# Which engine sums the channel blocks of the modulation vectors: one vector of a phase or all of them on the vector engine, and six raw buffers for seven

## The chip, the core and the metric

The kernel runs on one core of a Trainium2 chip. The core has five engines, each with an instruction stream of its own that it works through in order: PE (TensorE, matrix products into the accumulators in PSUM), DVE (VectorE) and ACT (ScalarE) (element-wise work), POOL (GpSimd), and SP (SyncE, which issues the transfers here). They wait for each other by semaphores. The metric is the device time of one launch in microseconds (us).

## What is computed

One denoising step of a two-layer network on 128 context tokens and 128 latent tokens with 1024 channels. All weights come from HBM once, some 300 MB. Per layer:

```python
x += 1/2 * gate1 * swiglu_1(mod1(rms_norm(x)))      # ffn1
u  = mod2(rms_norm(x)); z = u @ w_in                # mixer: attention, 2-D DFT, mLSTM on z,
x += gate2 * ((gated sum of the three branches) @ w_out)   # gates from u @ w_branch_gate
x += 1/2 * gate3 * swiglu_2(mod3(rms_norm(x)))      # ffn2

def adaln(cvec, w, b):                              # where shift, scale and gate come from
    m = jax.nn.silu(cvec) @ w + b                   # w: 1024 x 9216 per layer
    return jnp.split(m, 9, axis=-1)                 # nine vectors of 1024 channels
```

`adaln` is worked out for two condition vectors, one for the context tokens and one for the latent ones ("two groups" below). A modulation vector (layer l, number m) is therefore a product of a 2 x 1024 matrix with a 1024 x 1024 slice of `w_ada`, 4 MB of weights for two rows of result. There are 18 of them. The first two (shift and scale of the first phase) are worked out at the start and are not touched here; the other 16 are spread over the six phases, 3, 3, 3, 3, 3 and 1.

## The kernel before

**Steps and units.** The program is a list of steps that is written out by hand. A *unit* is a block of weights of 128 x 1024 numbers (some of 128 x 768). Products are made from two parts of each weight, so ACT rounds a unit to its high part (`whi`, line 1493) and DVE subtracts to get the low part (`wlo`, line 1494); that is the *split* of a unit. A step of PE takes one unit: 24 products of 256 columns (`mm3`, lines 168 to 170). There are six buffers for split units (`N_SPLIT`), and the executor at the end of the kernel writes, after each step, the split of the unit six further on: its buffer is free once PE is done with the unit of that step. Between steps DVE also multiplies the two halves of SwiGLU (line 655), makes the low part of the result (line 180), and in the mixer does most of the three branches ("lanes").

**Raw buffers.** Weights land in raw buffers of 1 MB (`N_RAW`, seven). SP issues the transfer of a block as soon as a buffer is given back; a block of weights is given back when both of its units are split.

**The modulation vectors.** `mod_steps` makes the steps for the vectors of one phase, and `spread_into` puts them evenly between two places of the step list. The steps of a phase lie in the first part of an ffn (products with `w_ffn_in`) and, in the mixer, between the second product of the first branch and the output product. Two ways are used:

- on PE (12 of the 16 vectors): a raw block of 2 x 128 channels by 1024 columns goes into the products as it is; four products of 512 columns run side by side, each into 32 rows of one PSUM tile (`pd`). One step takes two such blocks; a vector is two steps.
- on DVE (4 of the 16, one in each ffn, list `on_ve`): DVE multiplies a row block of 128 channels by the condition's number of that channel (one per partition, `cT`) and adds it to an accumulator (line 337 for the first block, line 339 for the other seven), one instruction for each group, 512 columns wide. Two halves of the columns make 16 pairs of instructions. Then PE sums the 128 partitions with a one-hot matrix (`hot`) in a step called `total`, one for each half.

After the last step of the phase ACT copies the PSUM tile (`adaev`), a step `post` transposes it and DVE adds the bias and makes gate, scale and shift.

Modulation steps carry no unit: where one stands between two unit steps, everything behind it on its engine waits until it is done. `acc[0]` is the accumulator; in the vector's last pair DVE writes it for the last time, and the products of `total` cannot start before that.

Units are numbered below over the whole program, in the order in which PE takes them: "behind unit 22" is the place after the 22nd unit that PE works through.

Of the kernel before, what the change touches and what calls it, by code (L numbers as in the profile page):

```python
# [17 lines left out]
P = 128  # L18
D = 1024
# [14 lines left out]
N_RAW = 7  # L34
N_SPLIT = 6
N_BLK = 17
N_T2 = 6
BRANCHES = (1, 0, 2)
CT = 8
HOT = 10  # L40
LAG = 2
# modulation vectors that each phase works out: those the vector engine sums first, and the others
ADA = {(0, "ffn1"): ([(0, 4)], [(0, 2), (0, 3)]),
       (0, "mixer"): ([], [(0, 7), (0, 6), (0, 5)]),
       (0, "ffn2"): ([(1, 1)], [(0, 8), (1, 0)]),
       (1, "ffn1"): ([(1, 4)], [(1, 2), (1, 3)]),
       (1, "mixer"): ([], [(1, 7), (1, 6), (1, 5)]),
       (1, "ffn2"): ([(1, 8)], [])}
# [31 lines left out]
def _pack(inputs):  # L80
    """Short vectors side by side, 128 wide, and the per-head gate biases and stabilisers."""
# [43 lines left out]
def trunk_kernel(ctx: ExitStack, tc: tile.TileContext, a: dict):  # L125
# [58 lines left out]
    # ---------------------------------------------------------------- small inputs  # L184
# [22 lines left out]
    # ---------------------------------------------------------------- persistent  # L207
# [36 lines left out]
    # ---------------------------------------------------------------- start-up  # L244
# [38 lines left out]
    def busy(n):  # L283
        """Products of nothing, which bring the tensor engine to its full clock while it has no data."""
        t = pb([P, 512])
        for _ in range(n):
            mm(t, zeros[:, 0:P], zeros)
# [10 lines left out]
    # ---------------------------------------------------------------- modulation  # L298
    def mod_steps(mods_):
        """Products of some modulation vectors.  # L300

        Four products run side by side: two quarters of the channels, two terms of their sums.
        Vector i takes the rows 2 i and 2 i + 1 of each. The vector engine first sums the channel
        blocks of those of the first list, one term per group, and the products sum its lanes."""
        on_ve, on_pe = mods_
        n_ve, mods_ = len(on_ve), on_ve + on_pe
        st = {"left": 4 * len(on_pe) + 2 * n_ve}
        seq = []

        def side(tiles, f0, f1):  # L310
            first = "ps" not in st
            if first:
                st["ps"] = pd([P, 512])
            st["left"] -= 1
            for q, (x, w) in enumerate(tiles):
                mm(st["ps"][32 * q:32 * q + 32, f0:f1], x, w, start=first, stop=st["left"] == 0)
            if st["left"] == 0:
                st["ev"] = t2([P, 512], "adaev")
                ac.copy(st["ev"], st["ps"])

        for i, (l, m) in enumerate(on_ve):
            for r in range(2):
                acc = []
                for jj in range(2):
                    f0 = m * D + r * 512
                    ch = Chunk(a["w_ada"][l, jj * 512:(jj + 1) * 512, f0:f0 + 512], 4, 512)
                    for e in range(4):
                        u = Unit(ch, e, e + 1, 0, 512, split=False)

                        def fn(u=u, k=4 * jj + e, acc=acc):  # L330
                            w = u.raw()[:, 0, :]
                            if k == 0:
                                acc.append(blk([P, 2, 512], "acc"))
                            for g in range(2):
                                c, x = cT[:, k, CT + g:CT + g + 1], acc[0][:, g, :]
                                if k == 0:
                                    ve.tensor_scalar(x, w, c, None, op0=ALU.mult)
                                else:
                                    ve.scalar_tensor_tensor(x, w, c, x, op0=ALU.mult, op1=ALU.add)  # L339

                        seq.append(((2 * i + r) * 8 + 4 * jj + e + 0.5, fn, [u]))

                def total(i=i, r=r, acc=acc):
                    side([(hot[:, HOT - 2 * i - g:HOT - 2 * i - g + 32], acc[0][:, g, c * 256:c * 256 + 256])
                          for g in range(2) for c in range(2)], r * 256, r * 256 + 256)

                seq.append(((2 * i + r) * 8 + 7.5 + LAG, total, []))
        span = 16 * n_ve if n_ve else 1
        for i, (l, m) in enumerate(on_pe):
            for j2 in range(2):  # L350
                us = []
                for j in range(2 * j2, 2 * j2 + 2):
                    ch = Chunk(a["w_ada"][l, j * 256:(j + 1) * 256, m * D:(m + 1) * D], 2, D)
                    us.append(Unit(ch, 0, 2, 0, D, split=False))

                def fn(us=us, i=n_ve + i, j2=j2):
                    for j, u in enumerate(us, 2 * j2):
                        raw = u.raw().rearrange("p e (r c f) -> p e c r f", r=2, c=2)
                        side([(cT[:, 2 * j + e, CT - 2 * i:CT - 2 * i + 32], raw[:, e, c])
                              for e in range(2) for c in range(2)], 0, 512)  # L360

                seq.append(((4 * i + 2 * j2 + 0.4) * span / (4 * len(on_pe)), fn, us))
        seq.sort(key=lambda x: x[0])
        out = [x[1:] for x in seq]

        def post():
# [3 lines left out]
            n = 2 * len(mods_)  # L370
            half = tmp([P, 2, 4, n], "mhalf", bufs=1)
            full = tmp([P, KD, n], "mfull", bufs=1)
            tq = t.rearrange("p c (q x) -> p q c x", x=32)[:, :, :, 0:n]
            ve.tensor_copy(half, tq[:, 0:2])
            for c in range(2):
                o = full.rearrange("p (r c b) x -> p c r b x", r=2, c=2)[:, c]
                i = (x.rearrange("p (r b) x -> p r b x", r=2) for x in (half[:, c], tq[:, 2 + c]))
                ve.tensor_add(o, *i)
            for i, (l, m) in enumerate(mods_):
                o, x = mods[l, m], full[:, :, 2 * i:2 * i + 2]  # L380
                bT = parT[l][:, m * KD:(m + 1) * KD].unsqueeze(2).to_broadcast([P, KD, 2])
                ve.tensor_add(o, x, bT)
                if m % 3 == 1:
                    k0 = 72 + m // 3 * KD
                    gT = parT[l][:, k0:k0 + KD].unsqueeze(2).to_broadcast([P, KD, 2])
                    ve.scalar_tensor_tensor(o, o, 1.0, gT, op0=ALU.add, op1=ALU.mult)
                elif m % 3 == 2 and m != 5:
                    ve.tensor_scalar(o, o, 0.5, None, op0=ALU.mult)
# [4 lines left out]
    # ---------------------------------------------------------------- norms  # L393
    class Norm:
        """Statistics and scaled copies of the residual, block by block.
# [1164 lines left out]
```

## Time and profile before

| | |
|---|---|
| median of 3 runs | 1375.77 us (1375.19 to 1377.95) |
| span of the profiled execution, first to last instruction | 1375.9 us |
| PE busy | 1351.3 us (98%) |
| DVE busy | 915.0 us (67%) |
| ACT busy | 682.3 us (50%) |
| DMA: moved, mean rate | 303.68 MB, 221 GB/s |
| mean granted TensorE clock | 0.990 of full speed |
| DVE, accumulating modulation vectors (lines 337 and 339) | 128 instructions, 85.9 us |
| PE, modulation products from raw weights in the phases | 384 rows of 512 columns, 46.2 us |

The profiled execution has no time of its own beside its span; the span lies inside the range of the timed runs. A product in full precision is two rows of the profile, so the four side-by-side products of a block are eight rows. Busy shares are averages over phases that differ: in the mixer DVE serves the branches as well as the splits, in the second half of an ffn it has little to do. The rows show a matmul as about 0.28 us long while the next starts about 0.12 us later, so durations of PE are read from starts, not from sums.

### The profile page before, as it was taken

What the parts mean: (1) busy time and instruction counts of PE and PEld (TensorE: products, weight loads), DVE (VectorE), ACT (ScalarE), POOL (GpSimd) and SP (SyncE); (2) the same over time, 40 slices, a digit from 0 to 9 for tenths busy, and PEclk for the clock granted to TensorE, in tenths of its full rate; (3) what the DMA queues carried; (4) which work ended last, traced back from release to release, by engine and by line L of the source; (5) the groups of instructions that cost most, each with busy time, mean ns of one, the idle gap of its engine ahead of it and who ended that gap; (6) DMA issues with size and microseconds to landing.
All of it is one profiled execution on the core that took longest, in us unless ns stands there. A gap on an engine that the chain in (4) does not pass through costs nothing.

```text
span 1375.9 us, 26101 instructions
## 1 busy us (share of the span) xinstructions
PE 1351.3 (98%) x10915; PEld 1268.7 (92%) x10916; DVE 915.0 (67%) x1440; ACT 682.3 (50%) x1096; POOL 113.0 (8%) x138
## 2 busy tenths in 40 slices
PE   6999999999999999999999999999999999999998
PEld 4999899888998999999998999998899899999998
DVE  4576755876557589666568666667665668887653
ACT  4544444666544466444455444546564445744442
POOL 2000001300000030000020000130000001200000
PEclk8999999999999999999999999999999999999999
DMA  9999856564468847886639876748445895487520
GB/s 293 333 345 340 260 174 213 159 195 138 157 238 298 272 154 267 300 269 212 206 124 321 305 257 197 204 130 241 154 137 195 297 304 186 147 264 233 192 85 31
DMA packets 247526, 303.68 MB, mean 221 GB/s; under 512 B 5537, under 2 KB 212657, under 8 KB 247409
## 3 DMA queue, kind: packets, MB, share of 16 engines
q1 hardware_dynamic: 245728, 296.98, 66.4%
q0 software_dynamic: 1680, 5.05, 1.1%
q8 instruction: 85, 1.39, 0.4%
q14 instruction: 33, 0.26, 0.1%
HBM read 297.80 MB, written 3.15 MB: 219 GB/s over the span
## 4 chain that ended last, share of the span: by engine, by line
PE 90%; DVE 6%; ACT 2%; DMA 1%; issue 1%; SPq 1%; POOL 0%; ACTq 0%; DVEq 0%
PE pm L168 26%; PE pm L170 25%; PE pm L169 25%; PE pd L165 5%; PE pb L165 2%; DVE wlo L1494 2%; DVE v L498 2%; DVE ul L180 1%; PE pm L752 1%; PE pm L754 1%; PE pm L753 1%; ACT whi L1493 1%; PE pa L165 1%; DMA raw<-w_ada 1%; PE pa L173 1%
## 5 line engine op out<-in xcount | busy, mean ns | idle before, releaser
L1494 DVE TENSOR_TENSOR wlo<-raw,whi 128x1024 fp32r<-128x1024 f32 (+1 forms) x424 | 507.3, 1204 | 326.4 <-ACT whi L1493 316.8
L1493 ACT CAST whi<-raw 128x1024 fp32r<-128x1024 f32 (+1 forms) x424 | 433.9, 1031 | 364.3 <-PE pm L169 253.4
L168 PE MATMUL pm<-uh,whi 128*128 128x256 f32 x1928 | 554.7, 288 | 0.0
L169 PE MATMUL pm<-ul,whi 128*128 128x256 f32 x1928 | 546.8, 284 | 1.7 <-DVE v L498 1.3
L170 PE MATMUL pm<-uh,wlo 128*128 128x256 f32 x1928 | 544.7, 283 | 3.2 <-DVE wlo L1494 3.2
L168 PEld LDWEIGHTS pm<-uh,whi 128*128 128x128 f32 x1928 | 366.8, 190 | 23.7 <-ACT whi L1493 9.1
L170 PEld LDWEIGHTS pm<-uh,wlo 128*128 128x128 f32 x1928 | 366.4, 190 | 4.4 <-DVE wlo L1494 4.4
L169 PEld LDWEIGHTS pm<-ul,whi 128*128 128x128 f32 x1928 | 366.2, 190 | 3.8 <-DVE v L498 1.7
L169 PE MATMUL pm<-hl,whi 128*128 128x256 f32 x704 | 197.9, 281 | 0.0
L168 PE MATMUL pm<-hh,whi 128*128 128x256 f32 x704 | 197.5, 281 | 0.0
L170 PE MATMUL pm<-hh,wlo 128*128 128x256 f32 x704 | 197.5, 281 | 0.0
L168 PEld LDWEIGHTS pm<-hh,whi 128*128 128x128 f32 x704 | 132.8, 189 | 0.0
L170 PEld LDWEIGHTS pm<-hh,wlo 128*128 128x128 f32 x704 | 132.7, 189 | 0.0
L169 PEld LDWEIGHTS pm<-hl,whi 128*128 128x128 f32 x704 | 132.6, 188 | 0.0
L423 POOL TENSOR_TENSOR nsum<-nsum,nsq 128x256 f32<-128x256 f32 x36 | 36.4, 1012 | 833.7 <-ACT nsq L421 833.7
L339 DVE SCALAR_TENSOR_TENSOR acc<-raw,cT,acc 128x512 f32<-128x512 f32 x112 | 78.9, 746 | 0.0
L165 PE MATMUL pd<-raw,cT 128*32 128x512 f32 (+1 forms) x512 | 56.5, 560 | 8.7 <-DMA raw<-w_ada 5.0
L653 ACT ACTIVATE silu<-pm 128x512 f32<-128x512 f32 x39 | 23.3, 597 | 69.5 <-PE pm L170 69.5
L165 PEld LDWEIGHTS pd<-raw,cT 128*32 128x32 f32 x512 | 14.0, 112 | 30.8 <-issue 20.4
L655 DVE TENSOR_TENSOR silu<-silu,pm 128x512 f32<-128x512 f32 x40 | 27.4, 685 | 22.6 <-PE pm L170 22.6
L568 DVE SCALAR_TENSOR_TENSOR xT<-pm,mod,xT 128x128 f32<-128x128 f32 x96 | 28.8, 342 | 18.1 <-PE pm L170 18.0
L1238 ACT ACTIVATE sig<-pm 128x512 f32<-128x512 f32 x24 | 14.4, 598 | 50.3 <-PE pm L170 50.1
(340 smaller groups left out, 1757.8 us busy)
## 6 DMA issues: line engine op xcount, KB each, us to landing
raw<-w_ffn_in SPq DMA_DIRECT2D x88, 1024.0 KB, 7.1
raw<-w_ada SPq DMA_DIRECT2D x64, 1024.0 KB, 6.0
raw<-w_ffn_out SPq DMA_DIRECT2D x32, 1024.0 KB, 7.1
raw<-w_in SPq DMA_DIRECT2D x32, 1024.0 KB, 5.9
raw<-w_branch_gate SPq DMA_DIRECT2D x24, 1024.0 KB, 5.4
raw<-w_ffn_out SPq DMA_DIRECT2D x16, 768.0 KB, 4.8
raw<-w_ada SPq DMA_DIRECT2D x16, 512.0 KB, 7.3
raw<-w_out SPq DMA_DIRECT2D x8, 1024.0 KB, 6.6
```

The costliest lines, as they stand in the source:

```text
L165: pe.matmul(out, lhsT, rhs, start=start, stop=stop)
L168: pe.matmul(out, sh, mh, start=start, stop=False)
L169: pe.matmul(out, sh, ml, start=False, stop=False)
L170: pe.matmul(out, sl, mh, start=False, stop=stop)
L339: ve.scalar_tensor_tensor(x, w, c, x, op0=ALU.mult, op1=ALU.add)
L423: eng.tensor_add(self.sum, self.sum, sq)
L498: ve.tensor_scalar(v[:, G[1]], v[:, G[1]], self.scale[:, k, 1:2], self.shift[:, k, 1:2], op0=ALU.mult, op1=ALU.add)
L568: ve.scalar_tensor_tensor(xT[:, k, G[g]], ps[:, G[g]], gate[:, k, g:g + 1], xT[:, k, G[g]], op0=ALU.mult, op1=ALU.add)
L653: ac.activation(st["s"], st["a"], AF.Silu)
L655: ve.tensor_mul(st["s"], st["s"], st["g"])
L1493: ac.copy(u.hi, r)
L1494: ve.tensor_sub(u.lo, r, u.hi.bitcast(F32))
```

## The change

All 16 vectors go the way of the one on DVE, and the rows become 1024 wide: a raw block now holds 2 x 128 channels by all 1024 columns of a vector, DVE works each of the two in a pair of instructions (one per group, two accumulators `acc0` and `acc1` of 1024 columns), and a vector is 8 steps with one pair each, one empty step, and one `total` with four products of 512 columns. The numbers of the conditions move to the front of `cT`, the one-hot matrix shrinks. `post` no longer adds two halves, since each quarter of the PSUM rows holds a group and a half of the columns. One raw buffer of 8 KB per partition is given up; one 4 KB block buffer (`N_BLK`) is added. Comments are dropped as well (not shown).

```diff
-N_RAW = 7
+N_RAW = 6
-N_BLK = 17
+N_BLK = 18
-CT = 8
-HOT = 10
-LAG = 2
-ADA = {(0, "ffn1"): ([(0, 4)], [(0, 2), (0, 3)]),
-       (0, "mixer"): ([], [(0, 7), (0, 6), (0, 5)]),
...
+CT = 0
+HOT = 4
+ADA = {(0, "ffn1"): [(0, 2), (0, 4), (0, 3)],
+       (0, "mixer"): [(0, 7), (0, 6), (0, 5)],
...
     def mod_steps(mods_):
-        on_ve, on_pe = mods_
...
+        st = {"left": len(mods_)}
+        out = []
+        for i, (l, m) in enumerate(mods_):
+            acc = []
+            for jj in range(4):
+                ch = Chunk(a["w_ada"][l, jj * 256:(jj + 1) * 256, m * D:(m + 1) * D], 2, D)
+                for e in range(2):
+                    def fn(u=Unit(ch, e, e + 1, 0, D, split=False), k=2 * jj + e, acc=acc):
+                        w = u.raw()[:, 0, :]
+                        for g in range(2):
+                            c = cT[:, k, CT + g:CT + g + 1]
                             if k == 0:
+                                acc.append(blk([P, D], f"acc{g}"))
+                                ve.tensor_scalar(acc[g], w, c, None, op0=ALU.mult)
+                            else:
+                                ve.scalar_tensor_tensor(acc[g], w, c, acc[g], op0=ALU.mult, op1=ALU.add)
+
+                    out.append((fn, [fn.__defaults__[0]]))
+
+            def total(i=i, acc=acc):
+                first = "ps" not in st
+                if first:
+                    st["ps"] = pd([P, 512])
+                st["left"] -= 1
+                for q in range(4):
+                    mm(st["ps"][32 * q:32 * q + 32, :], hot[:, HOT - i:HOT - i + 32],
+                       acc[q // 2][:, (q % 2) * 512:(q % 2 + 1) * 512], start=first, stop=st["left"] == 0)
+                if st["left"] == 0:
+                    st["ev"] = t2([P, 512], "adaev")
+                    ac.copy(st["ev"], st["ps"])
+
+            out += [(lambda: None, []), (total, [])]
...
+            tq = t.rearrange("p c (g h x) -> p g h c x", g=2, h=2)
             for i, (l, m) in enumerate(mods_):
...
+                for g in range(2):
+                    ve.tensor_add(o[:, :, g].rearrange("p (h c) -> p h c", h=2), tq[:, g, :, :, i],
+                                  bT.rearrange("p (h c) -> p h c", h=2))
```

DVE in the mixer of layer 0, from the second product of the first branch (`mg`) on, before: splits (`wlo`) and the work of the lanes.

```order
L1264 TENSOR_TENSOR mg_4151<-sig,pm 128x512
L1494 TENSOR_TENSOR wlo<-raw_3679,whi 128x1024
L1141 COPY nn<-pb 2x128 x2
L1494 TENSOR_TENSOR wlo<-raw_3739,whi 128x1024
L1156 SCALAR_TENSOR_TENSOR dn<-pb,gT 128x2
L1157 TENSOR_TENSOR dn<-dn,pb 128x2
L1158 RECIPROCAL dn<-dn 128x2
L1161 TENSOR_TENSOR ha<-pb,dn 128x256
L1494 TENSOR_TENSOR wlo<-raw_3739,whi 128x1024
```

The same place in the changed kernel (line numbers are 36 lower there; `acc_4192` and `acc_4194` are the accumulators of the two groups):

```order
L1228 TENSOR_TENSOR mg_4139<-sig,pm 128x512
L1458 TENSOR_TENSOR wlo<-raw_3727,whi 128x1024
L317 TENSOR_SCALAR acc_4192<-raw_3794,cT 128x1024
L317 TENSOR_SCALAR acc_4194<-raw_3794,cT 128x1024
L1105 COPY nn<-pb 2x128 x2
L1458 TENSOR_TENSOR wlo<-raw_3869,whi 128x1024
L319 SCALAR_TENSOR_TENSOR acc_4192<-raw_3794,cT,acc_4192 128x1024
L319 SCALAR_TENSOR_TENSOR acc_4194<-raw_3794,cT,acc_4194 128x1024
L1120 SCALAR_TENSOR_TENSOR dn<-pb,gT 128x2
L1121 TENSOR_TENSOR dn<-dn,pb 128x2
L1122 RECIPROCAL dn<-dn 128x2
L1125 TENSOR_TENSOR ha<-pb,dn 128x256
```

A pair of 1024-wide instructions now stands behind nearly every split of this stretch, 24 pairs in all, where there was none. In an ffn the pairs stand the same way between the splits; there were 16 pairs 512 wide in such a phase, and there are 24 pairs 1024 wide now (8 in ffn2 of layer 1).

PE in ffn1 of layer 0, the first modulation step, before (the products take the raw weights):

```order
L170 MATMUL pm<-uh_205,wlo 128x256
L165 MATMUL pd<-raw_639,cT 32x512 x4
L165 MATMUL pd<-raw_708,cT 32x512 x4
L168 MATMUL pm<-uh_204,whi 128x256
```

PE in the changed kernel, the first modulation step in the same phase:

```order
L169 MATMUL pm<-uh_202,wlo 128x256
L164 MATMUL pd<-acc_896,hot 32x512 x2
L164 MATMUL pd<-acc_898,hot 32x512 x2
L167 MATMUL pm<-uh_201,whi 128x256
```

Where PE read raw weights, two blocks to a step, it now reads the two accumulators, once for a vector. In units: the steps before that are seen in the rows below stand behind unit 15 (at 81.27 us), 41 (164.91), 116 (414.95), 128 (457.96), 150 (526.17), 158 (551.00) and 184 (631.92); the first pair of a phase stood behind unit 14 in ffn1 of layer 0, where it still does, and behind unit 150 in ffn2, where it now stands behind 148. In the changed kernel the eight pairs of the first vector stand behind units 14 to 20 and its `total` behind unit 22, those of the second behind 23 to 30 and 32, those of the third behind 33 to 40 and 42. In ffn2 of layer 0 the pairs stand behind units 148 to 157, 161 to 170 and 173 to 182, the totals behind 159, 172 and 185; in the mixer of layer 0 behind 106 to 113, 116 to 122 and 125 to 131, the totals behind 115, 124 and 133. Six split units ahead of PE are kept in all these stretches, as before. Layer 1 has the same pattern in its ffn1 (as ffn2 of layer 0) and its mixer; its ffn2 has one vector.

## Rows read from the trace of the kernel before

**Rows 1.** The page's first lines: span; busy time, share and instructions of an engine.

```profile
span 1375.9 us, 26101 instructions
...
PE 1351.3 (98%) x10915; PEld 1268.7 (92%) x10916; DVE 915.0 (67%) x1440; ACT 682.3 (50%) x1096; POOL 113.0 (8%) x138
```

**Rows 2.** Stretches: length, busy time by engine, granted clock, DMA share, GB/s.

```profile
377.80:472.20 94.40, 94.40 (x797) 84.77 (x797) 58.53 (x99) 40.50 (x68) 3.05 (x3) 1.00 0.82 281
...
80.20:165.00 84.80, 84.05 (x708) 77.00 (x708) 62.07 (x82) 37.52 (x43) 0.00 (x0) 1.00 0.91 309
...
526.10:632.00 105.90, 105.90 (x893) 99.07 (x896) 76.87 (x97) 48.93 (x61) 0.00 (x0) 1.00 0.88 296
```

**Rows 3.** Groups by shape: count, busy time, mean ns of one, idle before.

```profile
L1494 DVE TENSOR_TENSOR wlo<-raw,whi 128x1024 fp32r<-128x1024 f32 x392 | 476.7, 1224 | 323.0 <-ACT whi L1493 315.3 <-PE pb L165 5.4 <-PE pd L165 2.1
L1493 ACT CAST whi<-raw 128x1024 fp32r<-128x1024 f32 x392 | 407.2, 1047 | 330.1 <-PE pm L169 225.3 <-issue 86.9 <-PE pm L754 15.2
...
L339 DVE SCALAR_TENSOR_TENSOR acc<-raw,cT,acc 128x512 f32<-128x512 f32 x112 | 78.9, 746 | 0.0
...
L180 DVE TENSOR_TENSOR hl<-silu,hh 128x512 fp32r<-128x512 f32 x40 | 27.4, 685 | 0.0
```

**Rows 4.** DVE in order of time, ffn2 of layer 0: start, length, line.

```profile
532.08 0.88 DVE L337 TENSOR_SCALAR acc<-raw,cT 128x512 f32<-128x512 f32 x2
532.87 3.49 DVE L1494 TENSOR_TENSOR wlo<-raw,whi 128x1024 fp32r<-128x1024 f32 x3
...
539.94 1.22 DVE L1494 TENSOR_TENSOR wlo<-raw,whi 128x1024 fp32r<-128x1024 f32 x1
541.08 1.41 DVE L339 SCALAR_TENSOR_TENSOR acc<-raw,cT,acc 128x512 f32<-128x512 f32 x2
542.40 2.36 DVE L1494 TENSOR_TENSOR wlo<-raw,whi 128x1024 fp32r<-128x1024 f32 x2
```

**Rows 5.** The chain that ended last, modulation products: start, length, engine, tile.

```profile
81.27 1.85 PE pd L165 x16
...
164.91 0.62 PE pd L165 x4
...
414.95 1.85 PE pd L165 x16
...
457.96 1.86 PE pd L165 x16
...
526.17 1.85 PE pd L165 x16
551.00 1.85 PE pd L165 x16
...
631.92 0.57 PE pd L165 x8
```

**Rows 6.** DVE in order of time, ffn1 and mixer of layer 0.

```profile
80.03 1.23 DVE L1494 TENSOR_TENSOR wlo<-raw,whi 128x1024 fp32r<-128x1024 f32 x1 [2.17 <-ACT whi L1493]
...
378.89 1.23 DVE L1494 TENSOR_TENSOR wlo<-raw,whi 128x1024 fp32r<-128x1024 f32 x1 [0.28 <-ACT whi L1493]
```

**Rows 7.** PE at the start of the kernel, after three waits.

```profile
17.45 1.93 PE L165 MATMUL pd<-raw,cT 128*32 128x256 f32 x16 [3.51 <-DMA raw<-w_ada]
...
24.12 1.07 PE L165 MATMUL pd<-raw,cT 128*32 128x256 f32 x16 [1.02 <-DMA raw<-w_ada]
...
31.42 1.94 PE L165 MATMUL pd<-raw,cT 128*32 128x256 f32 x16 [3.67 <-DVE wlo L1494]
```

**Rows 8.** Single microseconds there; the third number from the end is the clock.

```profile
36.00:37.00 1.00, 1.00 (x6) 1.00 (x6) 0.35 (x1) 0.90 (x2) 0.00 (x0) 0.50 1.17 301
37.00:38.00 1.00, 1.00 (x9) 1.00 (x8) 0.43 (x1) 0.00 (x0) 0.00 (x0) 0.83 1.16 290
```

**Rows 9.** Transfers of modulation weights: count, size of one, us to landing.

```profile
raw<-w_ada SPq DMA_DIRECT2D x64, 1024.0 KB, 6.0
```

More of the change, by code (lines that the diff above doesn't have):

```diff
@@ L32 @@
 ATT_SCALE = 64.0 ** -0.5
-N_RAW = 7
+N_RAW = 6
 N_SPLIT = 6
-N_BLK = 17
+N_BLK = 18
 N_T2 = 6
 BRANCHES = (1, 0, 2)
-CT = 8
-HOT = 10
-LAG = 2
-ADA = {(0, "ffn1"): ([(0, 4)], [(0, 2), (0, 3)]),
-       (0, "mixer"): ([], [(0, 7), (0, 6), (0, 5)]),
[L45 to L48, printed above, removed]
+CT = 0
+HOT = 4
+ADA = {(0, "ffn1"): [(0, 2), (0, 4), (0, 3)],
+       (0, "mixer"): [(0, 7), (0, 6), (0, 5)],
+       (0, "ffn2"): [(0, 8), (1, 1), (1, 0)],
+       (1, "ffn1"): [(1, 2), (1, 4), (1, 3)],
+       (1, "mixer"): [(1, 7), (1, 6), (1, 5)],
+       (1, "ffn2"): [(1, 8)]}
 C_ID, C_BM, C_LO, C_CS, C_CD, C_SD, C_COS, C_SIN, C_MF, C_MB, C_END = (
@@ L299, in mod_steps @@
     def mod_steps(mods_):
-        on_ve, on_pe = mods_
[L306 to L331, printed above, removed]
-                            if k == 0:
[L333 to L362, printed above, removed]
@@ L363, in mod_steps @@
-        seq.sort(key=lambda x: x[0])
-        out = [x[1:] for x in seq]
+        st = {"left": len(mods_)}
[9 more added lines that the diff above has]
+                            c = cT[:, k, CT + g:CT + g + 1]
+                            if k == 0:
+                                acc.append(blk([P, D], f"acc{g}"))
[15 more added lines that the diff above has]
+            out += [(lambda: None, []), (total, [])]
@@ L369, in post @@
                 trans(t[:, c, :], st["ev"][:, c * P:(c + 1) * P])
[L370 to L378, printed above, removed]
+            tq = t.rearrange("p c (g h x) -> p g h c x", g=2, h=2)
             for i, (l, m) in enumerate(mods_):
-                o, x = mods[l, m], full[:, :, 2 * i:2 * i + 2]
-                bT = parT[l][:, m * KD:(m + 1) * KD].unsqueeze(2).to_broadcast([P, KD, 2])
-                ve.tensor_add(o, x, bT)
+                o, bT = mods[l, m], parT[l][:, m * KD:(m + 1) * KD]
+                for g in range(2):
+                    ve.tensor_add(o[:, :, g].rearrange("p (h c) -> p h c", h=2), tq[:, g, :, :, i],
+                                  bT.rearrange("p (h c) -> p h c", h=2))
                 if m % 3 == 1:
```

## Prediction, made before the changed kernel ran

> **What bounds the kernel now.** I read the page's first lines, then the chain of waits, then the stretches in which the modulation vectors are worked out, and last DVE in order of time. PE is busy 98% of the span and DVE 67% [rows 1]. In the stretches with modulation steps PE is busy throughout (94.4 of 94.4 us, 105.9 of 105.9) [rows 2], and its modulation products stand in the chain [rows 5], so what they take is on the path today. DVE has room on average only: in the mixer stretch it works 58.5 of 94.4 us without a single modulation instruction, in the two ffn stretches 62.1 of 84.8 and 76.9 of 105.9 us with one vector [rows 2]. These stretches decide, since the program order lets DVE work only some units ahead of PE or behind it.
>
> **What PE gives up.** Twelve vectors of two steps, 1.85 us each, are 44.4 us; eight `total` steps of 0.57 us are 4.6 us [rows 5]. What is added is 16 totals of four products 512 columns wide, half of a 1.85 us step: 0.93 us each, 14.8 us. PE loses 34.2 us of work that is on the path.
>
> **What DVE takes on.** No row has a 1024-wide accumulation. Starts tell more than durations: a pair 512 wide at 541.08 lets the next instruction start at 542.40, 1.32 us for two, 0.66 each; a 1024-wide subtraction takes 1.14 from start to start (539.94 to 541.08) [rows 4]. A two-tensor instruction grows by 1224 - 685 = 539 ns from 512 to 1024 columns [rows 3], so the 1024-wide accumulation is 0.66 + 0.54 = 1.20 us. Bounds: 0.66 us (the width costs nothing) and 1.32 us (it saves nothing) [rows 4]; I take 1.20, close to the 1024-wide subtraction, which has the same two tensors to read. The first block of a vector takes 0.79 us for two at 512 [rows 4], so 0.40 each, and I take 0.70 at 1024 (0.40 to 0.80). A vector is 14 x 1.20 + 2 x 0.70 = 18.2 us; before, in 512-wide rows, 28 x 0.66 + 4 x 0.40 = 20.1 us. So DVE gets 16 x 18.2 - 4 x 20.1 = 211 us more, and three vectors of a phase are 54.6 us.
>
> The Trainium skill has a rule against this way of saving, in "VectorE: DVE Perf Modes", section "Mode 2×_2P": an fp32 instruction with one tensor operand can run at twice the rate, one with two tensors cannot. Rows 4 agree: 0.40 against 0.66 us at 512 columns. So by the rule the width saves the fixed part alone, which is what 18.2 against 20.1 us says; with the page's figures for one element per cycle (some 1182 cycles at 0.96 GHz, 1.23 us, an estimate) a vector would be 0.4 us longer.
>
> **Where the two meet.** The products of `total` are in PE's order two modulation places behind the vector's last pair. PE cannot pass them, and behind them wait the units of the phase. DVE in turn cannot go on to the next vector: the split that stands ahead of its first pair needs a buffer which PE gives back with the unit behind the product. So each vector is a race between DVE's pairs and PE's units, and a lost race leaves DVE idle afterwards as well. Units take (551.00 - 526.17 - 1.85) / 8 = 2.87 us [rows 5].
>
> *ffn1 of layer 0.* DVE's own work is 62.1 - 20.1 = 42.0 us over 26 units, 1.6 per unit [rows 2]. The first pair can start at 80.03 + 1.14 = 81.2 [rows 6], where it starts now. Six more units of own work and the vector: 81.2 + 9.6 + 18.2 = 109.0. PE, at unit 15 at 81.27 [rows 5] and with no step to do there, is at the product behind unit 22 at 81.3 + 7 x 2.87 = 101.4 and waits 7.6 us. Then product 0.93, unit 2.87, the rounding of the split on ACT 1.05 [rows 3], seven units of own work 11.2 and the vector 18.2: 34.3 us to the next product, twice, so the third starts at 177.6 and ends at 178.5. Before, PE was done with unit 42 at 164.9 + about 0.6 + 2.87 = 168.4 [rows 5]: +10.
>
> *ffn2 of layer 0, ffn1 of layer 1.* The first pair starts at 532.1 [rows 4], held back by the end of the norm; PE is ahead by then: it ended unit 150 at 526.17 [rows 5]. Eight units of own work at 1.54 ((76.9 - 20.1 - 4.6 at the start) / 34 [rows 2]) and the vector: 562.6. PE is at the product at 526.2 + 9 x 2.87 = 552.0 and waits 10.6 us. From there the races are nearly even, since 13 units lie between two products (38.2 us against some 40.9, then 38.1): 2.7 us more. Third product done at 562.6 + 2 x 38.2 + 2.7 + 0.9 = 642.7; before, the same point was at 631.92 + 0.57 + 2.87 = 635.4 [rows 5]: +7 each.
>
> *Mixers.* The first pair starts at 378.89 + 1.14 = 380.0 [rows 6]; own work is 58.5 us over 25 units, 2.34 per unit [rows 2]. First product possible at 380.0 + 7 x 2.34 + 18.2 = 414.6; PE without its two steps is there at 414.95 - 3.7 - 2.87 = 408.4 [rows 5] and waits 6.2. Then 0.93 + 2.87 + 1.05 until the next split, 1.14 for it, 6 x 2.34 own, 18.2: 38.2 us, twice, 491.0, product done 491.9. Before, unit 133 ended at 457.96 + 1.86 + 5 x 2.87 = 474.2 [rows 5]: +18 each.
>
> ffn2 of layer 1 has one vector and room for it: 0.93 instead of 2 x 0.57 us. Sum: 10 + 2 x 7 + 2 x 18 = +60.
>
> **The clock.** After waits of 3.51 and 3.67 us PE came back at half speed (16 products in 1.93 and 1.94 us instead of 1.07); after 1.02 us it did not [rows 7]. The granted clock was still 0.50 (1.2 GHz of 2.4) at 36 to 37 us and rose in the next microsecond [rows 8]: from 31.4 to 37.3, so that some 3 us were lost. Of the waits above 11 are longer than 3.7 us: 7.6, 4.7 and 4.7 (34.3 less 0.93 and ten units) in ffn1 of layer 0, 6.2 and then some 9 and 11 in each mixer, and the first in each of the ffns between. The 3 us falls into the time in which DVE waits for the next unit, so it lengthens the race too: 34.3 becomes 37.3, 38.2 becomes 41.2, and 3 us follow the last product. ffn1 of layer 0: +19; the ffns between: +10 each; mixers: 414.6 + 2 x 41.2 + 3.9 = 500.9, +27 each. Sum 19 + 20 + 54 = +93.
>
> The Trainium skill ("TensorE: Matmul & The Clock Gate", section "HAM oscillation — how this bites in real kernels") says that a stream of products broken by a wait in each round starts each round with the throttled clock and pays each time. Rows 7 agree at this kernel's start. By the rule the sum is +93, without it +60.
>
> **The other edits.** `post` has about as many small DVE instructions as before: no term. The six raw buffers: a block of 1 MB lands in 6.0 us [rows 9]. In ffn1 of layer 0 the phase takes 28 blocks in some 107 us, one per 3.8 us, so a buffer comes round in 23 us; landing and two units of use are 6.0 + 7.6, and 9 us remain; in the mixer more. SP issues as many blocks of the same size as before. I count nothing; the cover is those 9 us, and without them the cost is that of the last rival.
>
> The execution profiled has a span of 1375.9 us, within the range of the timed runs, so sums are made on 1375.9 and hold for the median. Forecast: 1375.9 + 93 = 1469 us.
>
> **Rivals.**
> 1. *The waits come, the clock holds* (they are spread more evenly by the lanes, which also wait for DVE): 1376 + 60 = 1436. For it: the wait of 1.02 us that left the clock up. Against it: the two longer ones [rows 7]. If in addition DVE never idled between vectors, ffn1 of layer 0 would be 81.2 + 42.0 + 54.6 less 3 us of own work behind the last pair, +7, the ffns between +1 each, the mixers +18: 1421. Less than that DVE's own sum does not allow.
> 2. *Faster: the six units of lead cover DVE.* If `total` never waits, PE's 34.2 us come off: 1342. It needs own work plus 54.6 us to fit into the stretch: in the ffn 42.0 + 54.6 = 96.6 into 79 us of PE, in the mixer 58.5 + 54.6 = 113.1 into 86. Lead delays a shortage and does not remove 27 us; it would decide only if an accumulation cost under some 0.7 us, hardly more than a 512-wide one.
> 3. *Slower still: raw blocks come late.* DVE works in order and a late block holds up splits and branches alike. It decides from the point where a buffer's round is shorter than landing plus use (9 us to spare in ffn1 of layer 0). Price: 0.6 us for each of the 64 blocks, 38 us more, 1507; lanes on PE that wait for DVE's branch work inside a unit would cost about as much.
>
> **How the numbers follow.** Forecast 0.50, rival 1 0.35 (0.25 near 1436, 0.10 near 1421), rival 2 0.05, rival 3 0.10. The range 1412 to 1500 holds the forecast and rival 1 and leaves out the others. Between 1373 and 1378.5 (0.2%, what a measurement tells from no change) lies almost nothing: 0.01. Faster by more: 0.04. Slower by more: 0.95.
>
> **What would show it.** Right: accumulations 1024 wide at about 1.2 us from start to start; PE idle before the products of `acc`, released by DVE, 6 to 12 us at a time in the mixers, and a clock of 0.50 behind these waits; DVE near 90% busy or more in the mixer stretch and standing between two vectors for a split's rounding on ACT; the two mixers carrying more than half of the loss; the second halves of the ffns and ffn2 of layer 1 unchanged. Wrong: no PE wait at those products, a 1024-wide accumulation below 0.9 us, or DVE waiting for transfers of `raw`.

## Result, and the profile after

The changed kernel takes 1461.37 us (median of 4 runs, 1460.97 to 1462.84) against 1376.76 for the kernel before beside it: ratio 1.0617, 95% interval 1.0602 to 1.0632, so 84.6 us slower. The forecast was 1469 us. The time lands close, but two of its terms were wrong in opposite directions, as the runs below show, so that the closeness is in part luck.

The page's first lines and, from section 2, the clock by 40ths of the span, of the kernel after; they answer to [rows 1]:

```profile
span 1459.3 us, 25641 instructions
...
PE 1344.5 (92%) x10596; PEld 1266.7 (87%) x10596; DVE 1115.4 (76%) x1566; ACT 679.8 (47%) x1096; POOL 117.5 (8%) x138
...
PEclk9989999999998899899999899999999988999999
```

DVE is busy 200 us more (forecast 211). PE, idle for 2% of the span before, now stands idle for 8%. Groups by shape, as [rows 3]; the last column is the idle time just before the group and what ended it:

```profile
L319 DVE SCALAR_TENSOR_TENSOR acc<-raw,cT,acc 128x1024 f32<-128x1024 f32 x224 | 277.2, 1281 | 0.0
L164 PE MATMUL pd<-acc,hot 128*32 128x512 f32 x128 | 41.7, 861 | 73.8 <-DVE acc L319 73.0
```

Most of the new idle time of PE is where the forecast put it: 73.0 us in 12 waits before the products of `acc`, released by DVE's last accumulation, of some 90 us by which PE's idle time grew. In the mixers PE now also waits for results of the branches (total us, times, longest), which it did not before:

```profile
PE pb L164 <- DVE nB L1115: 7.1, 2, 3.6
PE pa L172 <- DVE on L859: 6.5, 2, 3.2
```

The next rows are totals of ffn1, of the mixer and of ffn2 of layer 0 in order of time (PE: start, length, line, tiles, count, idle before); the one at 424.98, the mixer's first, did not wait, nor did the last of ffn2:

```profile
104.59 3.11 PE L164 MATMUL pd<-acc,hot 128*32 128x512 f32 x8 [8.18 <-DVE acc L319]
141.44 3.08 PE L164 MATMUL pd<-acc,hot 128*32 128x512 f32 x8 [4.00 <-DVE acc L319]
...
424.98 2.25 PE L164 MATMUL pd<-acc,hot 128*32 128x512 f32 x8
466.98 3.12 PE L164 MATMUL pd<-acc,hot 128*32 128x512 f32 x8 [6.32 <-DVE acc L319]
506.59 3.12 PE L164 MATMUL pd<-acc,hot 128*32 128x512 f32 x8 [9.41 <-DVE acc L319]
...
597.41 3.12 PE L164 MATMUL pd<-acc,hot 128*32 128x512 f32 x8 [9.90 <-DVE acc L319]
639.70 2.25 PE L164 MATMUL pd<-acc,hot 128*32 128x512 f32 x8 [1.59 <-DVE acc L319]
678.89 2.21 PE L164 MATMUL pd<-acc,hot 128*32 128x512 f32 x8
```

DVE in order of time between the first and the second vector of ffn1 of layer 0 (as [rows 4, 6]):

```profile
105.64 2.36 DVE L1458 TENSOR_TENSOR wlo<-raw,whi 128x1024 fp32r<-128x1024 f32 x2
112.93 1.23 DVE L1458 TENSOR_TENSOR wlo<-raw,whi 128x1024 fp32r<-128x1024 f32 x1 [4.93 <-ACT whi L1457]
114.07 1.41 DVE L317 TENSOR_SCALAR acc<-raw,cT 128x1024 f32<-128x1024 f32 x2
115.40 0.68 DVE L619 TENSOR_TENSOR silu<-silu,pm 128x512 f32<-128x512 f32 x1
...
117.73 2.47 DVE L319 SCALAR_TENSOR_TENSOR acc<-raw,cT,acc 128x1024 f32<-128x1024 f32 x2
120.13 1.22 DVE L1458 TENSOR_TENSOR wlo<-raw,whi 128x1024 fp32r<-128x1024 f32 x1
```

An accumulation takes (120.13 - 117.73) / 2 = 1.20 us from start to start (forecast 1.20), the first block (115.40 - 114.07) / 2 = 0.67 (0.70). DVE then splits two units and stands idle 4.93 us until ACT has rounded the next one, as the forecast said of a lost race. The stretches with modulation steps, now longer, as [rows 2] (length; busy time of PE, PEld, DVE, ACT, POOL; clock, DMA share, GB/s); then two single microseconds behind the first total, as [rows 8]:

```profile
80.20:180.90 100.70, 83.60 (x642) 75.17 (x640) 92.05 (x95) 37.06 (x44) 0.00 (x0) 0.90 0.74 249
109.00:110.00 1.00, 1.00 (x7) 1.00 (x6) 0.00 (x0) 0.00 (x0) 0.00 (x0) 0.50 1.06 371
110.00:111.00 1.00, 1.00 (x9) 1.00 (x9) 0.00 (x0) 0.00 (x0) 0.00 (x0) 0.89 1.08 429
387.90:512.20 124.30, 101.69 (x768) 93.25 (x768) 113.35 (x149) 42.49 (x70) 5.71 (x4) 0.89 0.64 219
561.50:681.10 119.60, 107.86 (x868) 101.08 (x867) 109.74 (x115) 49.35 (x61) 0.00 (x0) 0.96 0.78 265
```

DVE's share in them is now 91 to 92%, PE's 82 to 90%. In the mixer DVE works 113.35 us; 58.5 of its own and 54.6 for three vectors were forecast.

The phases can be compared by the one POOL instruction that ends each norm. Before, the first phases end at

```profile
240.31 0.72 POOL L475 TENSOR_TENSOR rstd<-var,expo 128x2 f32<-128x2 f32 x1 [2.65 <-DVE var L473]
508.37 0.71 POOL L475 TENSOR_TENSOR rstd<-var,expo 128x2 f32<-128x2 f32 x1 [1.38 <-DVE var L473]
709.37 0.71 POOL L475 TENSOR_TENSOR rstd<-var,expo 128x2 f32<-128x2 f32 x1 [2.66 <-DVE var L473]
```

and after at

```profile
252.54 0.71 POOL L439 TENSOR_TENSOR rstd<-var,expo 128x2 f32<-128x2 f32 x1 [2.65 <-DVE var L437]
544.05 0.71 POOL L439 TENSOR_TENSOR rstd<-var,expo 128x2 f32<-128x2 f32 x1 [1.51 <-DVE var L437]
755.38 0.71 POOL L439 TENSOR_TENSOR rstd<-var,expo 128x2 f32<-128x2 f32 x1 [2.69 <-DVE var L437]
```

The mixer of layer 0, for example, grew by (544.05 - 252.54) - (508.37 - 240.31) = 23.4 us. All phases read in that way, us against before; the experiments' columns are explained below:

| phase | forecast: clock full, at half | after | clock held | later totals | hardly any sums | two in the ffns |
|---|---|---|---|---|---|---|
| start and ffn1, layer 0 | +10, +19 | +13.7 | +11.0 | +3.7 | -9.9 | -6.5 |
| mixer, layer 0 | +18, +27 | +23.4 | +23.6 | +19.8 | -9.6 | -0.7 |
| ffn2, layer 0 | +7, +10 | +10.3 | +9.0 | +1.3 | -6.0 | -3.0 |
| ffn1, layer 1 | +7, +10 | +10.8 | +9.3 | +1.9 | -6.0 | -3.0 |
| mixer, layer 1 | +18, +27 | +26.4 | +26.1 | +21.7 | -8.9 | -0.2 |
| ffn2, layer 1 | 0 | +0.2 | +0.2 | +0.6 | +0.2 | +0.7 |

The phases are counted from the norm at the start of the program. The first line carries the start of the kernel, which differs between profiles: the first modulation pair starts between 74.1 and 81.2 us, at 81.17 in before's, at 76.44 in after's and at 79.31 in the kernel with the clock held, whose program is the same as after's up to there but for a tile of zeros. From that pair on ffn1 grew by (252.54 - 76.44) - (240.31 - 81.17) = 17.0 us.

### The profile page after: what moved, and what is told of

It reads as the page before. It is cut to its first block, busy times and chain, and to the rows that moved or that the text cites. A ratio compares the mean times of both kernels' runs of the same rounds, so it can differ in the third digit from the quotient of the medians.

```text
span 1459.3 us, 25641 instructions
## 1 busy us (share of the span) xinstructions
PE 1344.5 (92%) x10596; PEld 1266.7 (87%) x10596; DVE 1115.4 (76%) x1566; ACT 679.8 (47%) x1096; POOL 117.5 (8%) x138
## 4 chain that ended last, share of the span: by engine, by line
PE 61%; DVE 29%; issue 5%; ACT 2%; DMA 1%; SPq 1%; POOL 0%; DVEq 0%; ACTq 0%
PE pm L167 17%; PE pm L169 17%; PE pm L168 17%; DVE acc L319 14%; DVE wlo L1458 7%; PE pd L164 3%; DVE v L462 2%; PE pb L164 2%; ACT whi L1457 1%; DMA raw<-w_ada 1%; DVE ul L179 1%; PE pm L716 1%; PE pm L718 1%; PE pm L717 1%; PE pa L164 1%
## 5 line engine op out<-in xcount | busy, mean ns | idle before, releaser
L319 DVE SCALAR_TENSOR_TENSOR acc<-raw,cT,acc 128x1024 f32<-128x1024 f32 x224 | 277.2, 1281 | 0.0
L164 PE MATMUL pd<-acc,hot 128*32 128x512 f32 x128 | 41.7, 861 | 73.8 <-DVE acc L319 73.0
L164 PEld LDWEIGHTS pd<-acc,hot 128*32 128x32 f32 x128 | 5.3, 126 | 91.5 <-DVE acc L319 91.2
L178 ACT CAST hh<-silu 128x512 fp32r<-128x512 f32 (+1 forms) x42 | 25.5, 610 | 111.7 <-DVE silu L619 111.7
L716 PE MATMUL pm<-whi,uh 128*128 128x512 f32 x96 | 39.3, 409 | 0.0
```

Of the source, the lines that this page charges most:

```text
L164: pe.matmul(out, lhsT, rhs, start=start, stop=stop)
L178: ac.copy(hi, src)
L319: ve.scalar_tensor_tensor(acc[g], w, c, acc[g], op0=ALU.mult, op1=ALU.add)
L716: pe.matmul(ps[g], xh[:, G[g]], wh, start=(k == 0), stop=False)
```

## Experiments

**How much the clock costs.** Products of zeros stand before the nine totals that waited 4.0 us or longer, and add nothing to the sums:

```diff
+                for _ in range(fill[i]):
+                    mm(st["ps"], zfill[:, 0:P], zfill, start=first, stop=False)
+                    first = False
                 for q in range(4):
```

> The changed kernel with products of zeros ahead of those totals that wait (34, 14 and 18 of them in ffn1 of layer 0, none, 25 and 39 in each mixer, 42 ahead of the first total in the two ffns between); they add nothing to the result and keep TensorE at work through most of each wait. My forecast's clock term (11 waits at 3 us each) expects 1461 - 33 = 1428 us. The rows of the changed kernel speak for less: a total's products last 3.1 us at the half clock and 2.25 at the full one, and the clock is back 0 to 2.4 us behind them, some 1.5 us lost at each of 8 waits: 1449 us. If the vector engine's sum alone decides and what the clock loses is hidden under it, 1459 to 1463. In all cases the granted clock should stay at 1.00 in these waits.

Measured: 1455.56 us, ratio 1.0575 (1.0555 to 1.0596), mean clock 0.988 after 0.963. PE in order of time:

```profile
107.46 2.25 PE L167 MATMUL pd<-acc,hot 128*32 128x512 f32 x8 [0.83 <-DVE acc L324]
142.30 2.25 PE L167 MATMUL pd<-acc,hot 128*32 128x512 f32 x8 [0.96 <-DVE acc L324]
...
425.07 2.25 PE L167 MATMUL pd<-acc,hot 128*32 128x512 f32 x8 [2.73 <-DVE acc L324]
...
467.22 2.08 PE L167 MATMUL pd<-acc,hot 128*32 128x512 f32 x8
...
506.45 2.25 PE L167 MATMUL pd<-acc,hot 128*32 128x512 f32 x8 [0.97 <-DVE acc L324]
```

The products of a total take 2.25 us, not 3.1, so PE does come back at full speed. In ffn1 the round from total to total is 142.30 - 107.46 = 34.84 us, against 36.85 in the changed kernel, and the next 35.76 against 36.59. The two rounds of the mixer of layer 0 in the changed kernel, and then with the products of zeros (the clock is the third number from the end):

```profile
424.98:466.98 42.00, 32.02 (x245) 29.84 (x244) 39.89 (x61) 15.05 (x27) 1.01 (x1) 0.94 0.59 201
466.98:506.59 39.61, 30.20 (x229) 27.32 (x229) 36.68 (x40) 12.70 (x16) 2.51 (x1) 0.84 0.68 238
...
425.07:467.22 42.15, 38.41 (x268) 33.35 (x269) 40.06 (x61) 15.20 (x27) 1.01 (x1) 0.92 0.60 201
467.22:506.45 39.23, 36.88 (x268) 30.12 (x268) 36.51 (x40) 12.55 (x16) 2.51 (x1) 1.00 0.69 240
```

In the second round the clock is held, 1.00 against 0.84, and the round is 0.4 us shorter (0.8 in layer 1, 39.19 against 40.02). The first tells nothing of the clock: it fell there as in the changed kernel, behind PE's wait of 3.5 us for `nB`, where no products of zeros stand. The clock gave back 5.8 us in all (the single runs of the two kernels lie 3.2 to 9.0 us apart). None of the three expectations was met: the forecast's 33 us and my 12 are too much, nothing is too little.

**How much DVE's time costs.** The accumulations take 512 columns only:

```diff
-                                ve.scalar_tensor_tensor(acc[g], w, c, acc[g], op0=ALU.mult, op1=ALU.add)
+                                x = acc[g][:, 0:512]
+                                ve.scalar_tensor_tensor(x, w[:, 0:512], c, x, op0=ALU.mult, op1=ALU.add)
```

> The changed kernel, but the accumulations add only the first 512 channels of each block (the first block is still 1024 wide); the modulation vectors lack their second halves' sums. Products, waits, transfers and buffers stay as they are; the vector engine loses 16 x 14 x 0.54 = 121 us. If the loss is the vector engine's time against TensorE's units, nearly all waits go and TensorE's 34 us come off the kernel before: 1335 to 1347 us. If the loss comes from the order itself (a total that waits for the vector engine at all, the handing over of buffers, the clock), most of it stays: above 1420.

Measured: 1375.79 us, ratio 0.9991 (0.9979 to 1.0003), between the two expectations. Waits of PE (total us, times, longest):

```profile
PE pd L164 <- DVE acc L320: 21.1, 7, 3.7
```

Of the 119 us between the changed kernel and the 1342 that a kernel without waits was to take, 85.6 went, but 21 us of waits stayed. I should have asked my own working: with 10.6 us a vector the first product of ffn2 of layer 0 comes at 532.1 + 8 x 1.54 + 10.6 = 555.0 and PE is there at 552.0, a wait of 3.0 us. The trace has 2.97:

```profile
548.04 2.02 PE L164 MATMUL pd<-acc,hot 128*32 128x512 f32 x8 [2.97 <-DVE acc L320]
```

Here, where PE and DVE are nearly even, a small wait costs the clock as well. The stretches around that of ffn1 of layer 1 (the clock is the third number from the end):

```profile
740.00:750.00 10.00, 6.89 (x51) 5.14 (x49) 10.00 (x14) 3.94 (x5) 0.00 (x0) 0.86 1.04 370
750.00:760.00 10.00, 10.00 (x68) 9.41 (x67) 4.35 (x5) 2.62 (x3) 0.00 (x0) 0.79 0.88 300
```

In this phase the wait and the clock took back all that PE had saved (-0.02 us against before); the mixers are 2.0 and 4.6 us longer than before even so. To settle what is left without any wait, 16 columns only:

```diff
-                                x = acc[g][:, 0:512]
+                                x = acc[g][:, 0:16]
```

(and the same for `w`.)

> The changed kernel, but each accumulation adds only 16 of 1024 channels, so the vector engine's part is nearly gone (the modulation vectors hold only the first block's products but for 16 channels); loads, order, products and buffers stay. It measures what TensorE gives up by itself: by the forecast 34.2 us come off, 1342 us (1338 to 1348), with no wait at a total. If the products in their new places cost more than counted, or a total costs even without a wait: above 1350.

Measured: 1337.44 us, ratio 0.9715 (0.9696 to 0.9734), 39 us under before, no wait at any total. The saving on PE is real, and a little larger than the 34.2 us counted: 8.9 to 9.6 in a mixer (8.3 counted: 6 x 1.85 - 3 x 0.93). So from here to the changed kernel DVE's accumulations alone cost 124 us.

**What a lost race costs.** Totals stand six places behind the last pair:

```diff
-            out += [(lambda: None, []), (total, [])]
+            out.append((8 * i + 7.5 + LAG, total, []))
+        n = 8 * len(mods_)
+        out += [(n + k, lambda: None, []) for k in range(LAG)]
+        out = [x[1:] for x in sorted(out, key=lambda x: x[0])]
```

with `LAG = 6`, and pairs numbered `8 * i + 2 * jj + e`.

> The changed kernel with each total six places behind its vector's last pair (now two), so behind the sixth pair of the next vector; the last vector's total has six empty places ahead of it, and the pairs stand closer. If a lost race leaves the vector engine idle afterwards (it waits for a buffer that TensorE gives back only behind the total), then a later total lets it work on: 1425 to 1442 us, with the idle time of the vector engine between vectors gone. If its sum alone decides and the idle time is unavoidable: 1455 to 1465. If the denser pairs hold up the splits: above 1465.

Measured: 1424.99 us, ratio 1.0354 (1.0338 to 1.0371), the lower end of the first theory and within 4 us of the 1421 that the forecast's first rival gave for a DVE that never idles. The ffns lose only 1.3 to 3.7 us, the mixers still 19.8 and 21.7. Waits of PE:

```profile
PE pb L173 <- DVE ha L1152: 38.1, 4, 10.4
PE pm L168 <- DVE silu L623: 23.2, 14, 3.8
```

No total waits any more. What PE waits for is DVE's ordinary work, which stands behind pairs. DVE in the mixer of layer 0:

```profile
423.48 4.86 DVE L320 SCALAR_TENSOR_TENSOR acc<-raw,cT,acc 128x1024 f32<-128x1024 f32 x4
428.26 0.69 DVE L1152 TENSOR_TENSOR ha<-ha,mss 128x512 f32<-128x512 f32 x1
```

`ha` starts right behind two pairs, on a DVE without a gap. From the first accumulation to the last of this mixer DVE works 102.59 of 106.20 us:

```profile
378.80:485.00 106.20, 82.48 (x653) 78.89 (x653) 102.59 (x139) 35.59 (x62) 7.24 (x4) 0.90 0.66 229
```

So the place of the total decides the loss in the ffns, and DVE's sum that of the mixers. The pairs also stand closer together in this run, which no run separates from the place of the totals.

**The mixers alone.** Their vectors go back to PE (the four quarters of the product's rows laid out as before, the rest as changed):

```diff
-       (0, "mixer"): [(0, 7), (0, 6), (0, 5)],
+       (0, "mixer"): ([], [(0, 7), (0, 6), (0, 5)]),
```

> The changed kernel with only the mixers' six vectors back on TensorE, as before the change (layout of the sums as before; rows 1024 wide and six raw buffers stay). In the changed kernel's trace the two mixer stages are 23.4 and 26.4 us longer than before. If the loss is local to the stage whose vectors are moved, 1461 - 50 = 1411 us (1406 to 1416). If part of the mixers' loss comes from the six buffers, or is handed on from the ffn ahead, 1420 or more.

Measured: 1415.79 us, ratio 1.0288 (1.0263 to 1.0313), the upper end of the local theory. The mixers change by -1.6 and +1.1 us against before, the ffns keep +14.8, +10.8 and +11.5. Each phase pays for its own vectors.

**The width.** The kernel before with all 16 vectors in its old lists for DVE:

```diff
-ADA = {(0, "ffn1"): ([(0, 4)], [(0, 2), (0, 3)]),
+ADA = {(0, "ffn1"): ([(0, 2), (0, 4), (0, 3)], []),
```

(and the other phases alike.)

> The kernel before with all sixteen later vectors summed on the vector engine by its old rows, 512 wide (two halves per vector, totals two places behind; seven raw buffers). A vector takes 20.1 us in place of 18.2 there, 30 us more in all. If the vector engine's time decides as in the changed kernel: 1461 + 30 less some 5 for the finer steps, 1480 to 1492 us. If the width saves nothing: 1458 to 1464.

Measured: 1526.87 us, ratio 1.1091 (1.1076 to 1.1105), well above both expectations. Waits of PE:

```profile
PE pd L165 <- DVE acc L339: 110.8, 28, 8.4
```

28 waits in place of 12: with two sums for a vector PE and DVE meet twice as often, and each meeting can idle both. I had taken the finer steps for a gain. Of the 65 us that the width is worth here, 30 are DVE's own time by the forecast's step (its busy time grows by 33.2, 1148.6 against 1115.4). I put the rest down to the meetings, which no run tests alone; DVE's idle time speaks for it, 17.8 of 121.6 us from the first to the last accumulation of ffn1 of layer 0, 8.6 of 102.7 in the changed kernel.

**The buffers.** Six and eighteen in the kernel before, and seven and seventeen in the changed one:

```diff
-N_RAW = 7
+N_RAW = 6
-N_BLK = 17
+N_BLK = 18
```

> The kernel before with six raw buffers and eighteen blocks, nothing else. The forecast counted nothing for it: 1374 to 1379 us. The kernels with six buffers reach their first pair 2 to 5 us earlier than the profiled run of before (76.4, 78.3, 79.0 and 79.3 against 81.2 us): if the buffers do that, 1372 to 1374. If a block comes late now and then, as my last rival has it: above 1379.

> The changed kernel with seven raw buffers and seventeen blocks, as before the change. By the forecast no difference: 1459 to 1463 us. If six buffers make blocks late in the crowded stages, it is faster: under 1457. If six buffers gain at the start: 1464 to 1466.

Measured: 1384.21 us, ratio 1.0059 (1.0047 to 1.0071), for the kernel before with six; 1461.55 us, ratio 1.0624 (1.0607 to 1.0641), for the changed one with seven. So in the changed kernel the buffer costs nothing, as forecast, but in the kernel before it costs 7.6 us. There a modulation step on PE takes two whole blocks at once. PE, at a place where the kernel before runs its 16 products without a stop (its row at 526.17 in [rows 5]):

```profile
527.74 1.07 PE L165 MATMUL pd<-raw,cT 128*32 128x512 f32 x8 [2.51 <-DMA raw<-w_ada]
```

By phase it loses 3.3 us in ffn2 of layer 0, 1.9 in ffn1 of layer 1 and 3.2 in the mixer of layer 1. Only the first two show such a wait (2.51 and 1.13 us), 3.6 of the 7.6 us; the rest stays open.

**A mix.** Rows 1024 wide, two of three vectors of the first three ffns and one of three of each mixer on DVE, totals four places behind:

```diff
+ADA = {(0, "ffn1"): ([(0, 4), (0, 2)], [(0, 3)]),
+       (0, "mixer"): ([(0, 7)], [(0, 6), (0, 5)]),
+       (0, "ffn2"): ([(0, 8), (1, 1)], [(1, 0)]),
...
+            seq.append((10 * i + 7.6 + LAG, total, []))
```

> A mix: rows 1024 wide and six raw buffers as in the changed kernel, but only two of three vectors of each of the first three ffns and one of three of each mixer are summed on the vector engine (ffn2 of layer 1 its one), each total four places behind its vector's last pair; the others are products on TensorE as before. The vector engine's sums fit: mixer 58.5 + 18.2 = 76.7 us into some 91, ffn between 52 + 36.4 = 89 into 103, ffn1 of layer 0 42.0 + 36.4 = 78.4 into 82. If that balance decides, TensorE saves 5 vectors x (3.70 - 0.93) and 4 x (1.14 - 0.93), 15 us: 1376.7 - 15 = 1362 us (1357 to 1367). If any total that waits for the vector engine costs by itself (as the kernel with half rows, 13 us of clock and waits on seven totals), 1370 to 1377.

Measured: 1380.89 us, ratio 1.0028 (1.0017 to 1.0038). My balance of averages was wrong for the mixers: +5.3 and +8.2 us, the ffns -4.5, -0.6 and -1.2. Two causes were left, so both were taken away, and then one:

```diff
-N_RAW = 6
+N_RAW = 7
-N_BLK = 18
+N_BLK = 17
...
-       (0, "mixer"): ([(0, 7)], [(0, 6), (0, 5)]),
+       (0, "mixer"): ([], [(0, 7), (0, 6), (0, 5)]),
```

> The mix without its two weak places: two of three vectors of each of the first three ffns on the vector engine in rows 1024 wide, totals four places behind, all mixers' vectors on TensorE, and seven raw buffers again. In the mix the three ffns were 4.5, 0.6 and 1.2 us shorter than before and the mixers 5.3 and 8.2 longer; six buffers alone made two of these ffns 3.3 and 1.9 longer. If these are the causes: ffns shorter by 4 to 6 us each and the mixers unchanged, 1360 to 1366 us. TensorE's own saving bounds it: 3 x 2.77 + 4 x 0.21 = 9.1, 1367.5. If the mixers' loss in the mix came from the ffn ahead, or the buffers don't matter here: 1370 to 1377.

> The mix of two and one vectors again, with seven raw buffers and seventeen blocks. It tells the two causes of the mixers' loss in the mix (5.3 and 8.2 us) apart. If the one vector on the vector engine costs it, where waits of TensorE for the vector engine's ha were 4.4 us: the mixers stay some 5 us longer each than before, 1365 + 10 = 1375 us (1372 to 1378). If the six buffers cost it: the mixers come out 3 us shorter than before, 1358 to 1362.

Measured: without both 1365.35 us, ratio 0.9920 (0.9906 to 0.9934), 11 us under the kernel before and as the first theory has it (though two of the three ffns gain 3.0 us, not 4 to 6). With seven buffers but the mixers' vector on DVE 1376.86, ratio 0.9993 (0.9981 to 1.0004): mixers +5.4 and +6.1, as the first theory has it. The vector costs this, although DVE has room on average: it works 54.9 of the 65.2 us from the first to the last accumulation. Waits of PE in that run:

```profile
PE pb L173 <- DVE ha L1182: 11.6, 4, 4.5
```

The mixer has a chain in which PE waits for DVE step by step, and a pair of 2.4 us in front of one of its steps is on the path. Here a pair stands ahead of `mss`, POOL works on that, DVE then makes `ha`, and PE waits:

```profile
437.77 2.48 DVE L334 SCALAR_TENSOR_TENSOR acc<-raw,cT,acc 128x1024 f32<-128x1024 f32 x2
...
440.76 0.17 DVE L1179 TENSOR_SCALAR mss<-mss 128x4 f32<-128x4 f32 x1
...
443.55 0.69 DVE L1182 TENSOR_TENSOR ha<-ha,mss 128x512 f32<-128x512 f32 x1 [0.90 <-POOL mss L1180]
...
444.30 1.11 PE L173 MATMUL pb<-cst,ha 128*128 128x128 f32 x4 [4.44 <-DVE ha L1182]
```

Neither the kernel before nor the run with all mixers' vectors on PE has such a wait.

## Why the prediction came out, step by step

**PE's part: right.** 34.2 us counted, 39 measured where DVE has next to nothing to do.

**DVE's part: right.** 1.20 us an accumulation, 18.1 a vector (14 x 1.20 + 1.33), 200 us in all against 211. The Trainium skill, "VectorE: DVE Perf Modes", section "Mode 2×_2P", has an fp32 instruction with one tensor operand at up to twice the rate of one with two. The trace agrees: the first block, with one, takes 0.67 us at 1024 columns and the accumulation, with two, 1.20.

**The race in the ffns: right.** Waits of 10.6, 2.7 and 0 us were forecast for ffn2 of layer 0, and 9.90, 1.59 and none measured; for ffn1 7.6, 4.7 and 4.7, and 8.18, 4.00 and 4.92. A round of ffn1 at full clock was to take 34.3 us, and the two took 34.84 and 35.76. In ffn2 the first was to take 40.9, a figure that stands in the forecast without its sum, and took 40.87. DVE's idle time between vectors is there, and moving the total takes it away.

**The mixers at full clock: the first step that failed.** "Then 0.93 + 2.87 + 1.05 until the next split, 1.14 for it, 6 x 2.34 own, 18.2: 38.2 us, twice". This follows one path, through the total and a buffer that comes free: it has DVE idle for the first 4.85 us and gives it 1.14 + 6 x 2.34 = 15.2 us of work of its own. Yet between two totals of a mixer stand nine units, and DVE has to serve all of them: 9 x 2.34 + 18.2 = 39.3 us by the forecast's own numbers. The round is the longer of the two. In ffn1 they are nearly even (ten units, 10 x 1.6 + 18.2 = 34.2 against 34.3 for the path), in the mixers DVE's sum is the longer. Measured are 42.00 and 39.61 us, with DVE at work for 39.89 and 36.68 of them (rows in the first experiment). Less the vector's 18.1 us, that is 21.8 and 18.5 us of its own work in place of 15.2, and 2.1 and 2.9 us of idle time in place of 4.85. The two rounds are 3.8 and 1.4 us longer than forecast and make the mixer +23 in place of +18; in the table it is +23.4. In layer 1 they are 41.97 and 40.02, +24 by the same sum against +26.4; the rest of that stays open.

**The clock: the second step that failed, by its size.** The clock is at half behind the nine waits of 4.0 us and longer, whose totals last 3.1 us, and up behind the three of 1.19 to 1.72, whose totals last 2.25. Eleven long waits were forecast: the first in each mixer, 6.2 us, did not come (none and 1.19); PE had already stood 3.2 us for `on` ahead of it. The "some 3 us" lost at each of 11 waits, 33 us, are 5.8. First, the 3 us were read at the kernel's start, where the clock was still at 0.50 5 us behind the first product [rows 7, 8]. At 104.59 it is as long at 0.50, but 2.25 us of that would have gone anyway to the wait for the second accumulator: the products last 3.11 in their place, and half of the 2.5 us up to 110.2 is lost behind them, 2.1 us in all; at 141.44 the clock is up again when they end. Second, I let the loss lengthen each round in full. It does so in the first round of ffn1, by 36.85 - 34.84 = 2.0 us; the second lost 0.8, and the first of ffn2 42.29 - 40.87 = 1.4. In the mixers, where DVE decides the round, most of it hides under DVE's work: 0.4 and 0.8 us in the rounds that can be compared. The Trainium skill ("TensorE: Matmul & The Clock Gate", section "HAM oscillation — how this bites in real kernels") has each round of a stream that a wait breaks start at the low clock and pay for it. In these rows that holds for the clock behind the nine waits, and only in part for the time: it says what PE loses, and how much of it the kernel loses depends on which engine sets the round.

So +93 was 60 + 33, and the runs show some 79 + 6: 27 us too much clock, 14 too little in the mixers, 5 too little in the ffns. The first error cancels most of the other two: that the total came within 8 us is in part luck.

**The buffers: right for this change.** Nothing was counted and nothing was lost. The cover was taken from the landing time, though, and not from how many blocks a step needs at once, which is how six buffers came to cost 7.6 us in the kernel before, as far as its two waits show.

**The rivals.** *The clock holds* (1436) stood on the mixers' mistake: with the clock held it is 1456. Its second form, a DVE that never idles (1421), is what later totals give (1425). *Faster* (1342) is what remains without DVE's work (1337), and half of that work already costs the whole gain. *Late raw blocks* did not come; of that rival's other half, lanes on PE that wait for DVE's branch work, 13.6 us did, the waits for `nB` and `on`. The forecast's sum counted nothing for them.

## What to carry to other kernels

Where two engines meet once a round, write down both sums for the round, the path through the meeting and all the work of the busier engine, counted over every unit of the round, and take the longer. What is lost off that engine costs little: a clock of 0.84 took 0.4 us of a round of 39.6. Work moved to an engine with idle time is free only where no short chain runs over it: two of three vectors in the ffns, in wide rows and with later totals, gained 11 us, while a single one in a mixer, with a sixth of DVE's time to spare, cost 5 to 6. And let a result be asked for late: four more places between the last sum and its product gave back 36 us, nearly as much as the 39 us of PE's work that the change saved.

## What was not expected of the hardware

Accumulating in rows of 512 rather than 1024 columns, the same data and the same sums with twice as many totals, costs 65 us (1526.87 against 1461.37), twice the 33 us by which DVE's busy time grows. The products of a total take 1.06 us where both accumulators are ready and 2.25 where the second is still being summed, both at full clock: PE's rows show the wait as length. PEld's show it as a wait (start, length, idle before; the kernel with the clock held, first total):

```profile
107.46 0.14 PEld L167 LDWEIGHTS pd<-acc,hot 128*32 128x32 f32 x4 [1.32 <-DVE acc L324]
108.66 0.14 PEld L167 LDWEIGHTS pd<-acc,hot 128*32 128x32 f32 x4 [1.05 <-DVE acc L324]
```
